# Token-major products in three passes instead of two, and the transposes of token block 1 a little later

## The chip, the core and the metric

The kernel runs on one core of one Trainium2 chip. The metric is device time in microseconds (us), from the first to the last instruction and what lies around them. Three runs of the kernel before took 1064.53, 1066.60 and 1066.75 us (median 1066.6).

## The reference

Two transformer blocks over 256 tokens of width 1024, in float32. The first has a gMLP mixer and a differential attention, each followed by a convolutional FFN; the second has a SwiGLU FFN, a mixer of MLA and block attention, and another SwiGLU FFN. Each of six stages begins with a normalised input that is multiplied by a weight:

```python
y = rmsnorm(h, norm_g[layer, 2])          # or rms_norm(x, g)
y = causal_dwconv(y @ w_up, conv_w, conv_b)   # or silu(y @ w_gate) * (y @ w_up), y @ w_in, ...
h = h + rmsnorm(y @ w_down, norm_g[layer, 3])
```

## The kernel before, in words

Tokens are in two blocks of 128 (tb 0 and 1). The weights come as 351 units of 128x1024 (512 KB each). Each float32 operand is split into a hi part and a lo part that TensorE takes at full speed, and a product is three matmuls: hi x hi (called HH here), hi x of the weights' lo (HL), and lo of x times hi of the weights (LH). A unit is prepared when it is called for: ScalarE writes its hi part `wh` (L304), VectorE its lo part `wl` (L310). `feed` prepares units ahead, up to W.ahead of them beyond those in use.

Between two stages lies `junction` (L573). For each token block it finishes the residual, forms the mean square, the norm `xn` (L510, two halves of 512 columns), turns `xn` on TensorE (L518, eight transposes into two tiles `pt`), and evicts the turned halves: ScalarE writes the hi part of `x` (L521), VectorE the lo part (L528). Token block 1 goes through this chain after token block 0, while TensorE already multiplies token block 0.

That multiplication is `token_major` (L409): the 8 chunks of 128 rows of x (k = 0 to 7) are the stationary operand, the weights stream, and the sums of one token block gather in two PSUM banks (`pz` in the FFNs, `accv` in the attention, `pmix` and `pckv` in the mixer). It returns a list of steps, one for each pass and each k, with a nominal time. `start` (L597) runs the steps of token block 0, then of token block 1, and calls `late` (the eight transposes of token block 1) at the first step at which the nominal time of the steps so far has reached TURN1.

Six stages begin in this way. They are numbered by their place in the trace: stage 1, the first FFN (82 us); stage 2, the differential attention (271 us); stage 3, the second FFN (382 us); stage 4, the third FFN (570 us); stage 5, the mixer (757 us); stage 6, the fourth FFN (869 us). An FFN's product is 768 columns wide, takes 6 units and 18 matmuls a pass; the attention's takes 8 units and 16 matmuls a pass; the mixer's 8 units and 16 matmuls a pass, then 2 more units for `pckv`. At the start of stages 2 and 5 six units are prepared, in stage 3 five of six, in stage 6, where W.ahead has been 4, two of six; the rest is prepared by instructions that stand behind the normalisation of token block 1 in ScalarE's and VectorE's queues.

Outside the stretches marked manual_schedule, as here, the order on each engine's queue is not that of the code: a planner places each instruction by its own estimate of when its inputs are ready, and the code's order only breaks ties. Instructions that write the same PSUM tile keep their order.

Of the kernel before, what the change touches and what calls it, by code (L numbers as in the profile page):

```python
# [56 lines left out]
k, v, q = (lambda c: ("k", c, 0)), (lambda tb: ("v", tb, 0)), (lambda h: ("q", h, 0))  # L57
# [172 lines left out]
def build(tc, nc, a, out):  # L230
    with ExitStack() as ctx:
        _build(ctx, tc, nc, a, out)


def _build(ctx, tc, nc, a, out):
# [10 lines left out]
    mm, act, vec = nc.tensor.matmul, nc.scalar.activation, nc.vector  # L246
# [121 lines left out]
    def block(x, tb, n=KD):  # L368

        return [(x[:, k, 0, TB[tb]], x[:, k, 1, TB[tb]]) for k in range(n)]  # L370
# [35 lines left out]
        vec.tensor_add(out_, hi, low)  # L406
        return out_

    def token_major(dst, xs, ws, n, major="pass"):  # L409

        last = len(xs) - 1
        res = []

        def one(k, passes):
            x = xs[k]
            segs = []
            for d, c0, c1 in dst:
                a0 = k * n + c0  # L420
                while a0 < k * n + c1:
                    a1 = min(k * n + c1, (a0 // D + 1) * D)
                    o = a0 - k * n - c0
                    segs.append((d[:, o:o + a1 - a0], a0 // D, slice(a0 % D, a0 % D + a1 - a0)))
                    a0 = a1
            for lr, hl in passes:
                for d, u, c in segs:
                    mm(out=d, lhsT=x[lr], rhs=ws(u)[hl][:, c], start=(k == 0 and lr == 0 and hl == 0), stop=(k == last and lr == 1))  # L428
        cols = sum(c1 - c0 for _, c0, c1 in dst)
        sets = ((((0, 0), (0, 1)), ((1, 0),)) if major == "pass" else (((0, 0), (0, 1), (1, 0)),))  # L430
        for passes in sets:
            for k in range(len(xs)):
                res.append((lambda k=k, passes=passes: one(k, passes), len(passes) * cols / 2400))
        return res
# [32 lines left out]
    def new_x():  # L467
        return xtp.tile([P, KD, 2, T], F32R, name=nm("x"), tag="x")
# [104 lines left out]
    def junction(proj, join, g):  # L573


        x = new_x()
        n0, n1 = [Norm(tb, proj.acc[tb], join, g, x) for tb in range(2)]
        n0.half(0, 1)
        n0.update()
        n0.scale()  # L580
        first, second = proj.rest()
        for f, _ in first:
            f()
        n1.half(0)
        cut_at = max(0.0, TURN0 - 0.64 * len(first))
        splice(second, [(cut_at, lambda: n0.turn(True))])
        n1.half(1)
        n1.update()
        n0.lo()
        n1.scale()  # L590
        return x, n1.turn

    QM = 2
    TURN0 = 7.0
    TURN1 = 5.0

    def start(x, late, groups):  # L597

        for tb in range(2):
            ops, done = groups(tb)  # L600
            t, turned = 0.0, tb == 1
            for f, us in ops:
                if not turned and t >= TURN1:
                    late()
# [10 lines left out]
    def ffn(x, late, evac, hooks):  # L615
# [6 lines left out]
        def groups(tb):  # L622
            pz = wide(tb, "pz")

            def done():
                zt = slot("z", shape=(P, n))
                for c0, c1 in parts:
                    act(zt[:, c0:c1], pz[c0 // 512][:, :c1 - c0], AF.Copy)
                z.append(zt)
            return token_major([(pz[c0 // 512][:, :c1 - c0], c0, c1) for c0, c1 in parts], block(x, tb), ws, n), done  # L630
# [240 lines left out]
    def diff_attention(x, late, bias, lam, sub, lam_work, mid):  # L871
# [3 lines left out]
        def groups(tb):  # L875
            acc = wide(tb, "accv")

            def done():
                vt = slot("vd")
                for q, c in enumerate(HALF):  # L880
                    act(vt[:, c], acc[q], AF.Copy)
                v.append(vt)
            return token_major([(acc[q], c.start, c.stop) for q, c in enumerate(HALF)], block(x, tb), ws, D), done
# [210 lines left out]
    def mixer(x, late, tables, mid):  # L1094
# [12 lines left out]
        def groups(tb):  # L1107
            pa = wide(tb, "pmix")
            pk = psm("pckv")
            ops = token_major([(pa[0], 0, 512), (pa[1][:, :416], 512, 928)], block(x, tb), w1, D)  # L1110
            ops += token_major([(pk[:, :T], 0, T)], block(x, tb), w2, T)

            def done():
                cn = slot("cn", shape=(P, 768))

                kr_, two = pa[1][:, 384:416], cn[:, 640:768].rearrange("p (r s d) -> p r s d", r=2, s=2)
                for s_, d, n, o in ((0, 0, 32, 0), (1, 0, 16, 16), (1, 16, 16, 0)):
                    vec.tensor_copy(two[:, :, s_, d:d + n], kr_[:, o:o + n].unsqueeze(1).to_broadcast([P, 2, n]))
                for ps, n, o in ((pa[1][:, :384], 384, 0), (pk[:, :T], 256, 384)):
                    ms = col("cms")  # L1120
                    act(cn[:, o:o + n], ps, AF.Square, accum_out=ms)
                    r = rsqrt_col(ms, mul=1.0 / n)
                    vec.scalar_tensor_tensor(out=cn[:, o:o + n], in0=ps, scalar=r, in1=cg[:, o:o + n], op0=ALU.mult, op1=ALU.mult)
                act(vals[1][:, tb, :], pa[0], AF.Copy)
                stage.append(cn)
            return ops, done
# [187 lines left out]
    x = new_x()  # L1314
# [5 lines left out]
    xs = [block(x, tb) for tb in range(2)]  # L1320
# [107 lines left out]
    x, late = junction(proj, held["post"], held["pre"])  # L1428
    hooks.append((MID, later(pre=lambda: norm_gain(1, 0), lam=lam_column, post=lambda: norm_gain(0, 3))))
    proj = ffn(x, late, conv_evac(held["cw"]), hooks)  # L1430
    x, late = junction(proj, held["post"], held["pre"])
    proj = diff_attention(x, late, rb["bias"], *held["lam"], later(pre=lambda: norm_gain(1, 2), cw=lambda: conv_taps(1), post=lambda: norm_gain(1, 1)))
    x, late = junction(proj, held["post"], held["pre"])
    proj = ffn(x, late, conv_evac(held["cw"]), [(MID, later(pre=lambda: gain(a["ffn1_norm"]), post=lambda: norm_gain(1, 3)))])
    x, late = junction(proj, held["post"], held["pre"])
    (step1, step2), tables = mixer_tables()
    proj = ffn(x, late, swiglu_evac, [(5, step1), (8, step2), (MID, later(pre=lambda: gain(a["mix_norm"]), cg=lambda: gain(a["cgain"], n=640)))])
    x, late = junction(proj, 0.5, held["pre"])
    proj = mixer(x, late, tables, later(pre=lambda: gain(a["ffn2_norm"])))
    x, late = junction(proj, 1.0, held["pre"])  # L1440
# [12 lines left out]
    for n, (c0, c1) in enumerate(ranges):  # L1453
        c, sum_ = slice(c0, c1), n < 2
# [16 lines left out]
    for c0, c1 in ranges[1:]:  # L1471
        c = slice(c0, c1)
# [47 lines left out]
```

## Time and profile before

| what | value |
|---|---|
| median of three runs (lowest, highest) | 1066.6 us (1064.53, 1066.75) |
| the profiled execution, its own time | 1064.43 us |
| span of that execution (first to last instruction) | 1062.6 us |
| TensorE busy in the span | 1047.2 us (99%) |
| TensorE's share of the chain that ended last | 93% |
| VectorE, ScalarE busy | 777.5 us (73%), 658.1 us (62%) |
| DMA, mean over the span | 185 GB/s |

The span and what lies around it make the execution's own time; the sum of the prediction is made against 1064.43. TensorE's busy time counts matmuls whose ends are modelled, so where one begins is better known than where it ends. An idle stretch of an engine is printed in brackets before the instruction that ended it, with the instruction that released it.

### The profile page before, as it was taken

To read this page: it belongs to the slowest core of one execution; us is meant where nothing else is said; L and a number is where in the kernel's file an instruction comes from. 1 tells how busy PE (TensorE), PEld (TensorE's weight loads), DVE (VectorE), ACT (ScalarE), POOL (GpSimd) and SP (SyncE) were. 2 spreads that over 40 slices of the span, in tenths; PEclk is the share of its full clock that TensorE was granted. 3 is DMA by queue.
4 is the path that set the end of the run, shared out by engine and by line. 5 is a ranking of instruction groups with operands and counts; after the bars stand their busy time and mean duration, and the time that the engine had idled before them with its cause. 6 is when DMAs were issued, how large, how long until landed. Compare 5 with 4: busy or idle time off the path is not lost.

```text
span 1062.6 us, 15791 instructions
## 1 busy us (share of the span) xinstructions
PE 1047.2 (99%) x5802; PEld 892.9 (84%) x5802; DVE 777.5 (73%) x1360; ACT 658.1 (62%) x1222; POOL 30.7 (3%) x57
## 2 busy tenths in 40 slices
PE   8999999999999999999999999999999999999997
PEld 6988888888788788888888888888898778888886
DVE  5886989887668877998876596665656867866633
ACT  6655867765578757876655575554457747755521
POOL 0100000000001110000001010000000000000000
PEclk9999999999999999999999999999999999999999
DMA  9956548653555446676534667564444456665501
GB/s 342 347 167 227 176 166 308 206 179 100 194 170 171 146 160 220 212 252 196 188 122 157 219 205 225 195 188 151 146 126 133 149 200 216 240 208 190 177 2 39
DMA packets 57246, 197.04 MB, mean 185 GB/s; under 512 B 6952, under 2 KB 9040, under 8 KB 57168
## 3 DMA queue, kind: packets, MB, share of 16 engines
q1 hardware_dynamic: 57024, 195.77, 55.8%
q8 instruction: 45, 0.74, 0.3%
q14 instruction: 33, 0.27, 0.1%
q10 hardware_dynamic: 144, 0.26, 0.1%
HBM read 194.94 MB, written 1.06 MB: 184 GB/s over the span
## 4 chain that ended last, share of the span: by engine, by line
PE 93%; DVE 2%; ACT 2%; DMA 1%; issue 1%; POOL 1%; SPq 0%; POOLq 0%; DVEq 0%; ACTq 0%
PE pu L385 26%; PE acc L544 26%; PE pu L384 12%; PE pz L428 5%; PE pq L385 4%; PE accv L1328 2%; PE pmix L428 2%; PE pq L384 2%; PE pu L387 2%; PE accv L428 2%; PE pt L518 1%; PE acc L1458 1%; PE pu L393 1%; PE pu L394 1%; PE pu L392 1%
## 5 line engine op out<-in xcount | busy, mean ns | idle before, releaser
L310 DVE TENSOR_TENSOR wl<-w,wh 128x1024 fp32r<-128x1024 f32 (+1 forms) x352 | 423.8, 1218 | 124.4 <-ACT wh L304 82.8
L385 PE MATMUL pu<-x,wh 128*128 128x512 f32 x1216 | 427.2, 396 | 0.0
L304 ACT ACTIVATE wh<-w 128x1024 fp32r<-128x1024 f32 (+1 forms) x352 | 362.1, 1051 | 94.2 <-DVE wl L310 62.9
L384 PE MATMUL pu<-x,wl 128*128 128x256 f32 x1064 | 296.7, 279 | 0.0
L385 PEld LDWEIGHTS pu<-x,wh 128*128 128x128 f32 x1216 | 222.7, 188 | 44.6 <-DVE y L682 0.6
L384 PEld LDWEIGHTS pu<-x,wl 128*128 128x128 f32 x1064 | 200.6, 189 | 6.6
L544 PE MATMUL acc<-wh,hh 128*128 128x512 f32 x434 | 145.4, 397 | 0.8 <-ACT hh L957 0.5
L544 PE MATMUL acc<-wl,hh 128*128 128x512 f32 x434 | 142.4, 390 | 0.0
L544 PE MATMUL acc<-wh,hl 128*128 128x512 f32 x434 | 141.4, 390 | 0.3 <-DVE hl L961 0.3
L399 ACT ACTIVATE low<-pu 128x256 f32<-128x256 f32 x152 | 57.4, 377 | 76.2 <-PE pu L385 75.3
L544 PEld LDWEIGHTS acc<-wh,hl 128*128 128x128 f32 x434 | 81.4, 188 | 18.3 <-DVE hl L961 0.9
L544 PEld LDWEIGHTS acc<-wl,hh 128*128 128x128 f32 x434 | 81.4, 188 | 17.0
L544 PEld LDWEIGHTS acc<-wh,hh 128*128 128x128 f32 x434 | 80.1, 188 | 16.1 <-ACT hh L437 1.4
L385 PE MATMUL pq<-x,wh 128*128 128x512 f32 x192 | 69.5, 403 | 0.0
L406 DVE TENSOR_TENSOR low<-pu,low 128x256 f32<-128x256 f32 x114 | 47.6, 418 | 17.8 <-ACT low L399 17.8
L428 PE MATMUL pz<-wh,x 128*128 128x256 f32 (+1 forms) x288 | 57.1, 321 | 0.0
L437 ACT ACTIVATE hh<-y 128x256 fp32r<-128x256 f32 x88 | 35.6, 409 | 29.8 <-DVE y L682 15.1
L670 ACT ACTIVATE y<-low,cw 128x256 f32<-128x256 f32 x76 | 45.0, 592 | 11.6 <-DVE low L406 11.2
L384 PE MATMUL pq<-x,wl 128*128 128x256 f32 x168 | 47.0, 279 | 0.0
L428 PEld LDWEIGHTS pz<-wh,x 128*128 128x128 f32 x288 | 42.5, 189 | 4.5 <-ACT x L521 0.3
L465 ACT ACTIVATE junk<-h 128x512 bf16<-128x512 f32 (+1 forms) x32 | 19.9, 622 | 40.3 <-DVE h L493 19.2
L438 DVE TENSOR_TENSOR hl<-y,hh 128x256 fp32r<-128x256 f32 x88 | 36.6, 420 | 9.8 <-ACT hh L437 9.7
(234 smaller groups left out, 1233.1 us busy)
## 6 DMA issues: line engine op xcount, KB each, us to landing
w<-in_wall SPq DMA_DIRECT2D x349, 512.0 KB, 4.4
gain<-in_norm_g SPq DMA_DIRECT2D x7, 512.0 KB, 6.7
h<-in_x SPq DMA_DIRECT2D x4, 256.0 KB, 5.5
w<-in_wall SPq DMA_DIRECT2D x4, 256.0 KB, 4.1
bias<-fd SPq DMA_DIRECT2D x2, 512.0 KB, 9.6
gain<-in_ffn_norm SPq DMA_DIRECT2D x2, 512.0 KB, 4.8
gain<-in_a_ln_g SPq DMA_DIRECT2D x1, 512.0 KB, 5.9
gain<-in_a_ln_b SPq DMA_DIRECT2D x1, 512.0 KB, 6.6
```

The lines of the kernel that those rows point to most:

```text
L304: act(self.hi[:, c], self.loaded[n][:, c], AF.Copy)
L310: vec.tensor_sub(wl[:, c], w[:, c], wh[:, c].bitcast(F32))
L384: mm(out=ps[:, T:], lhsT=wl, rhs=x[:, k, 0], start=False, stop=False)
L385: mm(out=ps, lhsT=wh, rhs=x[:, k], start=(k == 0), stop=(k == KD - 1))
L387: mm(out=ps[:, T:], lhsT=wl, rhs=x[:, k, 0], start=False, stop=False)
L399: act(low, ps[:, T:], AF.Copy)
L406: vec.tensor_add(out_, hi, low)
L428: mm(out=d, lhsT=x[lr], rhs=ws(u)[hl][:, c], start=(k == 0 and lr == 0 and hl == 0), stop=(k == last and lr == 1))
L437: act(hi, src, AF.Copy)
L438: vec.tensor_sub(lo, src, hi.bitcast(F32))
L544: mm(out=self.acc[tb][q], lhsT=hid[x][:, TB[tb]], rhs=w[hl][:, HALF[q]], start=s, stop=e)
L670: act(y, ps, AF.Identity, scale=cw[:, f, 2:3], bias=cw[:, f, 3:4])
```

## The change

The two sets of passes (HH and HL together for each k, then LH) become three: HH for all k, LH for all k, HL for all k. The flag that ends a sum goes to the last HL instead of the last LH. The unused argument of `token_major` goes. TURN1 goes from 5.0 to 5.5.

```diff
-    def token_major(dst, xs, ws, n, major="pass"):
+    def token_major(dst, xs, ws, n):
...
             for lr, hl in passes:
                 for d, u, c in segs:
-                    mm(out=d, lhsT=x[lr], rhs=ws(u)[hl][:, c], start=(k == 0 and lr == 0 and hl == 0), stop=(k == last and lr == 1))
+                    mm(out=d, lhsT=x[lr], rhs=ws(u)[hl][:, c], start=(k == 0 and lr == 0 and hl == 0), stop=(k == last and hl == 1))
         cols = sum(c1 - c0 for _, c0, c1 in dst)
-        sets = ((((0, 0), (0, 1)), ((1, 0),)) if major == "pass" else (((0, 0), (0, 1), (1, 0)),))
-        for passes in sets:
+        for passes in (((0, 0),), ((1, 0),), ((0, 1),)):
             for k in range(len(xs)):
                 res.append((lambda k=k, passes=passes: one(k, passes), len(passes) * cols / 2400))
...
-    TURN1 = 5.0
+    TURN1 = 5.5
```

A step now holds one pass over one k (nominally 0.32 us in an FFN, by `cols / 2400`), where a step of HH and HL held two. So the call of `late` moves, in the code, from behind 8 steps of 0.64 to behind 18 of 0.32 in the FFNs, from 6 of 0.853 to 13 of 0.427 in the attention, and from 7 of 0.773 to 15 of 0.387 in the mixer. In the three kinds of stage that is 0.64, 0.43 and 0.39 us of nominal work later. Where the transposes come in TensorE's queue is the planner's choice. Before, it followed the code in stages 1, 2, 4 and 5. Now it does so in stages 1 and 4 alone: before behind 36 matmuls (HH and HL of all k), now behind 41 (HH, LH and the first 5 of HL).

TensorE's queue in stage 2, around the transposes of token block 1 (`pt`, from `xn`); `accv` with an even and an odd number are the two halves of the columns, a `wh` or `wl` is one unit. Before, behind 24 matmuls (HH and HL for k = 0 to 5):

```order
L428 MATMUL accv_2960<-wl_602_2834,x_2851 128x512
L428 MATMUL accv_2961<-wl_602_2834,x_2851 128x512
L428 MATMUL accv_2960<-wh_604_2847,x_2851 128x512
L428 MATMUL accv_2961<-wh_604_2847,x_2851 128x512
L428 MATMUL accv_2960<-wl_605_2849,x_2851 128x512
L428 MATMUL accv_2961<-wl_605_2849,x_2851 128x512
L518 MATMUL pt_2986<-ident,xn_2957 128x128 x4
L518 MATMUL pt_2987<-ident,xn_2957 128x128 x4
L428 MATMUL accv_2960<-wh_638_3002,x_2851 128x512
```

Now, behind 12 (HH alone, for k = 0 to 5), with HH of k = 6 (the seventh unit, `wh_636`) between the third and the fourth transpose:

```order
L428 MATMUL accv_2960<-wh_601_2832,x_2851 128x512
L428 MATMUL accv_2961<-wh_601_2832,x_2851 128x512
L428 MATMUL accv_2960<-wh_604_2847,x_2851 128x512
L428 MATMUL accv_2961<-wh_604_2847,x_2851 128x512
L517 MATMUL pt_3000<-ident,xn_2957 128x128 x3
L428 MATMUL accv_2960<-wh_636_2976,x_2851 128x512
L428 MATMUL accv_2961<-wh_636_2976,x_2851 128x512
L517 MATMUL pt_3000<-ident,xn_2957 128x128
L517 MATMUL pt_3001<-ident,xn_2957 128x128 x4
L428 MATMUL accv_2960<-wh_639_2984,x_2851 128x512
```

The transposes stand 12 matmuls earlier in the queue than before. Stage 5 has the same pattern: before behind 28 matmuls of `pmix`, now three of them behind 12, and the rest two matmuls later.

TensorE's queue in stage 3, in the same place; `wh_949` is the hi part of the sixth unit. Before, behind 30 matmuls of `pz`:

```order
L428 MATMUL pz_4194<-wh_914_4073,x_4091 128x512
L428 MATMUL pz_4194<-wl_915_4075,x_4091 128x512
L518 MATMUL pt_4238<-ident,xn_4191 128x128 x3
L428 MATMUL pz_4195<-wh_949_4227,x_4091 128x256
L428 MATMUL pz_4194<-wh_949_4227,x_4091 128x512
L518 MATMUL pt_4238<-ident,xn_4191 128x128
L518 MATMUL pt_4239<-ident,xn_4191 128x128 x4
L428 MATMUL pz_4195<-wl_950_4229,x_4091 128x256
```

Now, the first three behind 15; the other five come 26 matmuls later, behind the rest of HH, all of LH and 5 of HL:

```order
L428 MATMUL pz_4195<-wh_914_4073,x_4091 128x256
L428 MATMUL pz_4194<-wh_914_4073,x_4091 128x512
L517 MATMUL pt_4243<-ident,xn_4191 128x128 x3
L428 MATMUL pz_4195<-wh_949_4213,x_4091 128x256
L428 MATMUL pz_4194<-wh_949_4213,x_4091 128x512
L428 MATMUL pz_4195<-wh_949_4213,x_4091 128x256
L428 MATMUL pz_4194<-wh_868_3908,x_4091 128x512
```

The first three transposes have moved 15 matmuls towards the front of the queue.

TensorE's queue in stage 6 now, where two units are prepared at the start (`wh_1989`, `wh_1995`); `pz_9194` and `pz_9195` are token block 0, `pz_9329` and `pz_9330` token block 1:

```order
L428 MATMUL pz_9194<-wh_1995_9104,x_9115 128x256
L428 MATMUL pz_9195<-wh_1995_9104,x_9115 128x256
L428 MATMUL pz_9194<-wh_1995_9104,x_9115 128x512
L517 MATMUL pt_9263<-ident,xn_9191 128x128 x4
L517 MATMUL pt_9264<-ident,xn_9191 128x128 x4
L428 MATMUL pz_9329<-wh_1989_9075,x_9115 128x512
L428 MATMUL pz_9330<-wh_1989_9075,x_9115 128x256
```

They stand behind 6 matmuls of HH; before, behind 12 (the same 6 and 6 of HL). Behind them now come 6 of HH for token block 1 and then, unit by unit, 3 of token block 0 and 3 of token block 1 for the third, fourth and fifth unit, with HL of both blocks last; before, HH and HL of each unit stood side by side.

ScalarE's and VectorE's queues in these stages keep their order but for two places: in stage 3 two preparations (L304, L310) now stand ahead of the evictions of token block 1 (L521, L528), and in stage 5 one stands behind them. From stage 6 on, some evictions of the fourth FFN change places with a neighbour. POOL's and SP's queues keep their order.

## Rows read from the trace of the kernel before

**Rows 1.** The page: busy time, share of the span and instructions of each engine.

```profile
PE 1047.2 (99%) x5802; PEld 892.9 (84%) x5802; DVE 777.5 (73%) x1360; ACT 658.1 (62%) x1222; POOL 30.7 (3%) x57
```

**Rows 2.** The waits of TensorE in the whole span: who waited for whom, us in total, times, the longest.

```profile
PE pt L518 <- DVE xn L510: 4.7, 6, 1.6
...
PE pz L428 <- DVE wl L310: 0.4, 1, 0.4
```

**Rows 3.** The time line of TensorE in stage 2: start, us, instruction, count, and in brackets the idle time before it.

```profile
270.80 0.62 PE L428 MATMUL accv<-wh,x 128*128 128x512 f32 x2
...
273.52 0.62 PE L428 MATMUL accv<-wh,x 128*128 128x512 f32 x2
...
275.79 0.61 PE L428 MATMUL accv<-wl,x 128*128 128x512 f32 x2
276.86 1.29 PE L518 MATMUL pt<-ident,xn 128*128 128x128 f32 x8 [0.46 <-DVE xn L510]
```

**Rows 4.** The time line of ScalarE, then of VectorE, in stage 2.

```profile
274.96 1.99 ACT L304 ACTIVATE wh<-w 128x1024 fp32r<-128x1024 f32 x2
...
275.96 1.41 DVE L510 SCALAR_TENSOR_TENSOR xn<-h,rs_r,gain 128x512 f32<-128x512 f32 x2 [0.66 <-POOL rs_r L460]
```

**Rows 5.** The time line of TensorE in stage 3.

```profile
381.56 0.50 PE L428 MATMUL pz<-wh,x 128*128 128x512 f32 x2
...
386.04 0.40 PE L428 MATMUL pz<-wl,x 128*128 128x512 f32 x1
387.54 0.55 PE L518 MATMUL pt<-ident,xn 128*128 128x128 f32 x3 [1.10 <-DVE xn L510]
387.84 0.60 PE L428 MATMUL pz<-wh,x 128*128 128x256 f32 x2
...
389.33 0.39 PE L428 MATMUL pz<-wl,x 128*128 128x256 f32 x1 [0.35 <-DVE wl L310]
```

**Rows 6.** The time line of ScalarE, then of VectorE, in stage 3.

```profile
385.72 1.99 ACT L304 ACTIVATE wh<-w 128x1024 fp32r<-128x1024 f32 x2
...
386.73 1.41 DVE L510 SCALAR_TENSOR_TENSOR xn<-h,rs_r,gain 128x512 f32<-128x512 f32 x2 [0.66 <-POOL rs_r L460]
```

**Rows 7.** The time line of stage 5: TensorE, ScalarE, VectorE.

```profile
757.39 0.57 PE L428 MATMUL pmix<-wh,x 128*128 128x512 f32 x2
...
759.91 0.58 PE L428 MATMUL pmix<-wh,x 128*128 128x512 f32 x2
...
763.28 1.04 PE L518 MATMUL pt<-ident,xn 128*128 128x128 f32 x8
...
759.01 2.94 ACT L304 ACTIVATE wh<-w 128x1024 fp32r<-128x1024 f32 x3
...
760.01 1.41 DVE L510 SCALAR_TENSOR_TENSOR xn<-h,rs_r,gain 128x512 f32<-128x512 f32 x2 [0.67 <-POOL rs_r L460]
```

**Rows 8.** The time line of stage 6: TensorE, ScalarE, VectorE.

```profile
868.62 0.50 PE L428 MATMUL pz<-wh,x 128*128 128x512 f32 x2
...
870.27 0.40 PE L428 MATMUL pz<-wl,x 128*128 128x512 f32 x1
872.29 1.29 PE L518 MATMUL pt<-ident,xn 128*128 128x128 f32 x8 [1.63 <-DVE xn L510]
873.61 0.61 PE L428 MATMUL pz<-wh,x 128*128 128x512 f32 x2
...
873.45 1.05 ACT L304 ACTIVATE wh<-w 128x1024 fp32r<-128x1024 f32 x1
...
874.88 8.64 ACT L304 ACTIVATE wh<-w 128x1024 fp32r<-128x1024 f32 x9
...
871.39 1.41 DVE L510 SCALAR_TENSOR_TENSOR xn<-h,rs_r,gain 128x512 f32<-128x512 f32 x2 [0.73 <-POOL rs_r L460]
```

**Rows 9.** The time line of TensorE: the transposes of token block 0 in stage 1, then the end of HH and HL of token block 0 and the transposes of token block 1, in stage 1 and in stage 4.

```profile
80.96 0.63 PE L518 MATMUL pt<-ident,xn 128*128 128x128 f32 x4 [1.04 <-DVE xn L510]
...
87.89 0.51 PE L428 MATMUL pz<-wl,x 128*128 128x512 f32 x2
88.62 1.29 PE L518 MATMUL pt<-ident,xn 128*128 128x128 f32 x8 [0.22 <-DVE xn L510]
...
575.72 0.51 PE L428 MATMUL pz<-wl,x 128*128 128x512 f32 x2
576.49 1.29 PE L518 MATMUL pt<-ident,xn 128*128 128x128 f32 x8 [0.26 <-DVE xn L510]
```

**Rows 10.** The time line of stage 1: VectorE's lo parts of x for token block 0, and ScalarE's hi parts of x for token block 1.

```profile
82.26 1.36 DVE L528 TENSOR_TENSOR x<-pt,x 128x512 fp32r<-128x512 f32 x2 [0.18 <-ACT x L521]
...
89.28 1.26 ACT L521 ACTIVATE x<-pt 128x512 fp32r<-128x512 f32 x2 [0.58 <-PE pt L518]
```

**Rows 11.** The instructions of L428: operation, count, shortest, median and longest duration in ns, first and last start, form.

```profile
L428 PEld LDWEIGHTS pz<-wh,x x288: 186/188/192, 82.3 to 888.4; 128*128 128x128 f32 x144
...
L428 PEld LDWEIGHTS pz<-wl,x x144: 186/188/192, 82.8 to 885.6; 128*128 128x128 f32 x144
```

**Rows 12.** Busy time by stretch: the stretch, its length, busy us and instructions of PE, PEld, DVE, ACT and POOL, then TensorE's granted clock (1.00 is its full speed), DMA share and GB/s. The wait in stage 6, and two stretches at the end of the program.

```profile
870.67:872.29 1.62, 0.00 (x0) 0.03 (x1) 0.90 (x2) 0.00 (x0) 0.55 (x1) 1.00 0.85 349
1058.00:1060.00 2.00, 0.00 (x0) 0.00 (x0) 0.88 (x2) 0.72 (x1) 0.40 (x1) 1.00 0.10 32
1060.00:1062.60 2.60, 0.00 (x0) 0.00 (x0) 0.00 (x0) 0.00 (x0) 0.00 (x0) 0.51 0.47 177
```

## The prediction

> **What bounds the kernel.** I read the page first: TensorE is busy 1047.2 of 1062.6 us [rows 1]. So hardly anything counts but the gaps on TensorE, and the next view is the list of its waits [rows 2]. The transposes of L518 waited for `xn` six times, 4.7 us in all, the longest 1.6 us, and L428 once for a lo part, 0.4 us. These are the only waits that the change can touch. The third view is the time line of each of the six stages; the reader is to see in it when TensorE comes to the transposes of token block 1 and when `xn` lets them start. The fourth is the order of the queues in the changed program, because the time line shows that the queue is kept. In stage 3 the transposes stand as three, two matmuls, then five, and so they run: after 1.10 us of idling, three transposes at 387.54, then the matmuls, though the hi part which these need came from a conversion that began at 385.72 [rows 5, 6].
>
> **What the change does not move.** The matmuls are the same in number and shape. `xn` of token block 1 comes from VectorE, ScalarE and POOL, whose order up to there is unchanged and which wait for nothing in the product of token block 0. So the transposes cannot start earlier than now: every matmul that leaves the front of them is idle time, and every one that comes in front of them fills idle time. From the start of the second norm to the first transpose takes 0.90 us in stage 2 (275.96 to 276.86) [rows 3, 4] and 0.90 us in stage 6 (871.39 to 872.29) [rows 8].
>
> **Stages 1 and 4: a gain.** The queue puts 5 more matmuls (0.70 us by the spacing below) ahead of the transposes. The last two before them start at 87.89 and at 575.72; two of 256 and 512 columns take some 0.35 us to the next start, so TensorE was free at 88.24 and 576.07 and lost 0.38 and 0.42 us [rows 9]. Both are less than 0.70, so both go: **-0.8 us**. What could be late next is x of token block 1: its evictions begin at 89.28, 0.66 us after the first transpose [rows 9, 10], and 13 matmuls of HL (some 2 us) still lie ahead of its first user. LH, now second, begins where the last 18 of the 36 matmuls did, some 2.8 us (18 at 0.157) before 88.24, and the lo parts of token block 0 that it needs are done at 83.68 [rows 10]. In the other stages the transposes move to the front, and x of token block 1 with them.
>
> **Stage 2: a loss.** Before, 24 matmuls lie ahead; the first starts at 270.80, the thirteenth at 273.52, the last pair at 275.79 [rows 3]. Now only 12 lie ahead, so TensorE comes to the transposes at 273.52 and waits to 276.86. The 12 others (2.72 us) come later, when nothing is left to hide: **+2.7 us**. HH of the seventh unit, between the transposes, is free of waits: two hi parts are converted from 274.96 in 1.99 us [rows 4].
>
> **Stage 3: a loss.** 30 matmuls run from 381.56 to about 386.27 (the last starts at 386.04) [rows 5], 4.71 us; half of them now lie ahead of the first three transposes: TensorE comes to these at 383.9 instead, and they start at 387.54 as before: **+2.35 us**. The wait of 0.35 us for the sixth lo part goes, because HL is last: **-0.35 us** [rows 5]. The hi part of that unit, wanted directly behind the three transposes, is ready (two conversions from 385.72, 1.99 us) [rows 6]. The five transposes that now come 26 matmuls later have their `xn` long since. The two conversions that pass the evictions on ScalarE and VectorE cost nothing, for those evictions wait for the late fifth to eighth transposes anyway.
>
> **Stage 5: a loss.** Before there is no wait at 763.28 [rows 7]. Now TensorE comes to the transposes behind 12 matmuls, at 759.91; the second norm begins at 760.01 and releases them 0.90 us on, at 760.91: **+1.0 us**. The seventh and eighth hi parts are converted from 759.01 on, three in 2.94 us, and meet their matmuls [rows 7].
>
> **Stage 6: a loss, and a new wait.** 12 matmuls run from 868.62 to about 870.50, of which 6 now stand ahead: half of 1.88 us is added to the idle 1.63 us, **+0.94 us** [rows 8]. Behind the transposes (to 873.6) come 6 matmuls of token block 1 (0.94 us, to 874.55), for which the third unit's hi part is done at 874.50; its 6 matmuls run to 875.48. The next three hi parts are done at 875.93, 876.88 and 877.83 (nine from 874.88 in 8.64 us, 1.05 us the last, so 0.95 us apart) and each feeds 6 matmuls of 0.93 us: TensorE waits 0.45 us for the first and next to nothing for the others, **+0.5 us**. Before, HH and HL of a unit took twice as long, which hid this. By its bounds this term is between 0 (a hi part somewhat earlier) and 1.5 us (all three late by as much).
>
> **What is not seen.** In token block 1 the lo parts of the shared units are now read to the end, so buffers for later weights come free later, by at most the 2.9 us of one pass. Nothing in the rows prices that; the bound below is 0, above it is one wait like the 0.4 us for a lo part [rows 2] in each of four FFNs, 1.6 us. I take 0, for the wait list has no wait behind such a load in these stretches.
>
> At the weight loads a rule speaks against the change. The rows: 288 loads of x for 288 matmuls with `wh` and 144 for 144 with `wl`, 188 ns each at the median [rows 11]; a second matmul with the same chunk of x loads it again, so parting HH from HL costs no load: 0. The Trainium skill, TensorE: Matmul & The Clock Gate, section on what each phase is for, says that weights are to be loaded once and multiplied repeatedly. By it, HL as a pass of its own would want 8 more loads for each token block of a stage, 96 in all, some 18 us by an estimate with 188 ns, were none hidden; the trace disagrees with its premise here.
>
> **The sum.** -0.8 + 2.7 + 2.35 - 0.35 + 1.0 + 0.94 + 0.5 = +6.3 us. On the profiled execution's 1064.4 us that is 1070.7. The median shown, 1066.6, lies 2.2 us above that execution, and one of the three runs beside it; a new median can fall in either place, 1070.7 or 1072.9, and I take **1072.0**.
>
> **The rivals.**
> *TensorE goes on past a waiting transpose.* Then the places in the queue mean little, the matmuls behind fill the gaps, and what decides is whether 0.4 us or more of work is ready when the transposes are not. The waits for `xn` of token block 1 would shrink to nothing: -3.7 us (4.7 less 1.04 for token block 0 in stage 1 [rows 2, 9]) and -0.4, that is 1060.3, faster. For it: such work is in the queue in all six stages. Against it: in stage 3 TensorE idled 1.10 us with a matmul behind the transposes whose hi part was done at about 386.8 [rows 5, 6]. 5 in 100.
> *TensorE's clock falls in the longer gaps.* The gaps of stages 2 and 3 come to 3.3 and 3.6 us, twice the longest now. In the rows the clock stays at its full 2.4 GHz through the idle 1.6 us of stage 6 and still in 1058 to 1060, when the last matmul is over, and reads 0.51, that is 1.2 GHz, in the last 2.6 us, in which TensorE did nothing either [rows 12]. At the lower level the matmuls behind a gap take twice as long; no row shows how long that lasts. Between 0 and doubling the 7.7 us that token block 0 has left in stage 2 (34 matmuls of 0.227), I put 3 us on each of two gaps: 1078. The same page of the skill, section on why this matters for your kernels, warns of idle gaps between bursts of matmuls, behind which the clock is lower; in the gaps of this trace that does not show. 5 in 100.
> *The change does not do what its words say, yet costs nothing,* because `xn` is not what ends the waits: were the transposes released by TensorE's own earlier work, they would move with it. Then only small terms are left, within 2 us of 1066.6. Against it: each wait ends 0.90 us behind the second norm's start. 6 in 100.
> *More waits for weights* in stage 6 and for buffers, at the upper bounds: +2.6 us more, 1074.6. 9 in 100.
>
> **How the numbers follow.** My forecast has 75 in 100. A measurement tells 0.2%, 2.1 us, from no change. Slower by more: 75 + 5 + 9 = 89. Within: 6. Faster: 5. For the range: the terms that rest on a row each way are good to some 0.7 us in all, the median's place to 2.2 us, so the forecast alone lies between 1069.5 and 1074; taking in the bounds above, 1069.0 to 1075.5. The clock, the second rival, is left out of it, and so are most of the two milder ones.
>
> **What would show it.** Right: the wait of L518 for `xn` grows from 4.7 to about 11 us in all, in four long pieces (about 3.2 in stage 2, 3.5 in stage 3, 0.9 in stage 5, 2.6 in stage 6), with 1.0 left in stage 1 and none in stage 4; the wait of L428 for a lo part is gone, and one of some 0.5 us for a hi part stands in stage 6. TensorE's busy time stays near 1047. Wrong: transposes that start earlier than 0.9 us behind the second norm, matmuls that run between the arrival at the transposes and their start, or a granted clock under 1.00 behind a gap.

## The result, and the profile after

The changed kernel takes **1074.3 us** (median of four runs, 1072.87 to 1076.22) beside 1065.6 of the kernel before on the same chip. The ratio is 1.0082, 95% interval 1.0070 to 1.0094: slower by 8.7 us. The forecast was 1072.0, its range 1069.0 to 1075.5. The profiled execution took 1072.87 us, its span is 1071.1; before, 1064.43 and 1062.6.

The page first. TensorE's row, to be held against [rows 1]:

```profile
PE 1050.2 (98%) x5802; PEld 897.1 (84%) x5802; DVE 777.7 (73%) x1360; ACT 657.0 (61%) x1222; POOL 31.8 (3%) x57
```

The span grew by 8.5 us and TensorE's busy time by 3.0, with as many instructions; so 5.5 us are idle time and 3.0 are matmuls that took longer. The waits of TensorE (us in total, times, the longest) show the first part:

```profile
PE pt L517 <- DVE xn L509: 11.1, 5, 3.5
```

11.1 us instead of the 4.7 of [rows 2], and the wait for a lo part is gone from the list. The time line of TensorE shows where: stage 1 (the view ends after the first four matmuls of HL), then stages 2, 3, 5 and 6 (L517 is L518 of before; the idle time ahead of an instruction is in brackets).

```profile
88.45 1.03 PE L517 MATMUL pt<-ident,xn 128*128 128x128 f32 x8
89.24 0.95 PE L428 MATMUL pz<-wl,x 128*128 128x512 f32 x4
...
269.67 2.88 PE L428 MATMUL accv<-wh,x 128*128 128x512 f32 x12
275.74 0.87 PE L517 MATMUL pt<-ident,xn 128*128 128x128 f32 x3 [3.18 <-DVE xn L509]
276.26 1.20 PE L428 MATMUL accv<-wh,x 128*128 128x512 f32 x2
...
384.04 2.51 PE L428 MATMUL pz<-wh,x 128*128 128x512 f32 x15
390.01 0.55 PE L517 MATMUL pt<-ident,xn 128*128 128x128 f32 x3 [3.45 <-DVE xn L509]
390.31 5.06 PE L428 MATMUL pz<-wh,x 128*128 128x256 f32 x21
...
765.99 0.52 PE L517 MATMUL pt<-ident,xn 128*128 128x128 f32 x3 [0.84 <-DVE xn L509]
...
878.40 1.52 PE L517 MATMUL pt<-ident,xn 128*128 128x128 f32 x8 [2.59 <-DVE xn L509]
879.71 8.70 PE L428 MATMUL pz<-wh,x 128*128 128x512 f32 x45
```

The idle pieces in stages 2, 3, 5 and 6 are 3.18, 3.45, 0.84 and 2.59 us; the forecast had 3.2, 3.5, 0.9 and 2.6. What the forecast did not have is the pace behind them. In stage 3 the 21 matmuls take 5.06 us, where 0.157 each would be some 3.5 with the end of the last. The stretches say why (stretch, its length, TensorE's busy us and instructions, granted clock, DMA share, GB/s):

```profile
274.00:275.00 1.00, 0.00 (x0) 1.00 0.46 160
275.00:276.00 1.00, 0.27 (x2) 0.58 0.85 315
276.00:277.00 1.00, 1.00 (x5) 0.50 0.34 139
...
390.00:391.00 1.00, 0.99 (x7) 1.00 0.00 0
391.00:392.00 1.00, 1.00 (x7) 0.60 0.00 0
392.00:393.00 1.00, 1.00 (x5) 0.50 0.00 0
393.00:394.00 1.00, 1.00 (x6) 0.50 0.37 45
394.00:395.00 1.00, 1.00 (x6) 0.69 0.52 193
395.00:396.00 1.00, 1.00 (x9) 1.00 0.74 299
```

The granted clock goes from 1.00 to 0.50, that is from 2.4 to 1.2 GHz, inside the gap of stage 2 (TensorE starts again at 275.74) and 1.2 us behind the gap of stage 3, and comes back. Stage 6 shows the same (0.50 in 880 to 882, 0.82 in 882 to 884). In the profile of before nothing of the kind stands behind a gap of these stages.

A table of my own condenses the time lines. For each execution it has the time from the first matmul of token block 0 to the first instruction behind the whole product, in us, by stage:

| profiled execution | 1 | 2 | 3 | 4 | 5 | 6 | sum |
|---|---|---|---|---|---|---|---|
| before | 18.53 | 23.76 | 19.76 | 18.54 | 26.85 | 20.14 | 127.6 |
| after | 17.87 | 27.39 | 23.04 | 17.88 | 27.88 | 22.47 | 136.5 |
| e1, the passes alone | 18.55 | 26.07 | 23.08 | 18.54 | 27.89 | 22.23 | 136.4 |
| e2, TURN1 alone | 17.88 | 24.11 | 19.81 | 17.88 | 27.00 | 21.68 | 128.4 |
| e3, gaps filled | 17.90 | 26.02 | 21.54 | 17.88 | 27.88 | 21.52 | 132.7 |
| e4, HH and LH paired | 17.85 | 23.11 | 19.17 | 17.83 | 26.84 | 20.14 | 124.9 |
| e5, all three per k | 17.78 | 23.10 | 17.82 | 17.87 | 26.84 | 19.21 | 122.6 |
| e6, order of the code | 17.89 | 27.02 | 20.88 | 17.88 | 27.67 | 21.94 | 133.3 |
| e7, eight units ahead | 17.94 | 24.14 | 17.87 | 17.88 | 26.96 | 20.18 | 125.0 |
| e9, before with a filled gap | 18.53 | 23.79 | 19.81 | 18.54 | 26.84 | 19.91 | 127.4 |

From before to after the six products grow by 8.95 us. Between them nothing moved: from the end of one to the start of the next it is 169.71, 87.00, 169.10, 168.43 and 84.38 us before, and 169.73, 86.98, 169.08, 168.43 and 84.37 after. (The first stage began 0.5 us earlier in the profiled execution of after, which makes 8.5.)

### The profile page after: what moved, and what is told of

Same layout as the page of the kernel before. It is cut to its first block, busy times and chain, and to the rows that moved or that the text cites. A ratio compares the mean times of both kernels' runs of the same rounds, so it can differ in the third digit from the quotient of the medians.

```text
span 1071.1 us, 15789 instructions
## 1 busy us (share of the span) xinstructions
PE 1050.2 (98%) x5802; PEld 897.1 (84%) x5802; DVE 777.7 (73%) x1360; ACT 657.0 (61%) x1222; POOL 31.8 (3%) x57
## 4 chain that ended last, share of the span: by engine, by line
PE 94%; DVE 2%; ACT 2%; POOL 1%; issue 1%; DMA 0%; SPq 0%; POOLq 0%; DVEq 0%; ACTq 0%
PE pu L385 26%; PE acc L543 26%; PE pu L384 12%; PE pz L428 6%; PE pq L385 4%; PE accv L1327 2%; PE accv L428 2%; PE pq L384 2%; PE pmix L428 2%; PE pu L387 2%; PE pt L517 1%; PE acc L1457 1%; PE pu L393 1%; PE pu L392 1%; PE pu L394 1%; ACT junk L464 1%
## 5 line engine op out<-in xcount | busy, mean ns | idle before, releaser
L310 DVE TENSOR_TENSOR wl<-w,wh 128x1024 fp32r<-128x1024 f32 (+1 forms) x352 | 423.9, 1219 | 128.9 <-ACT wh L304 88.5
L304 ACT ACTIVATE wh<-w 128x1024 fp32r<-128x1024 f32 (+1 forms) x352 | 361.9, 1051 | 97.5 <-DVE wl L310 63.9
L543 PE MATMUL acc<-wh,hh 128*128 128x512 f32 x434 | 145.4, 397 | 0.8 <-ACT hh L956 0.5
L543 PE MATMUL acc<-wl,hh 128*128 128x512 f32 x434 | 142.4, 390 | 0.0
L543 PE MATMUL acc<-wh,hl 128*128 128x512 f32 x434 | 141.4, 390 | 0.3 <-DVE hl L960 0.3
L543 PEld LDWEIGHTS acc<-wh,hl 128*128 128x128 f32 x434 | 81.4, 188 | 18.2 <-DVE hl L960 0.9
L543 PEld LDWEIGHTS acc<-wl,hh 128*128 128x128 f32 x434 | 81.4, 188 | 17.0
L543 PEld LDWEIGHTS acc<-wh,hh 128*128 128x128 f32 x434 | 80.1, 188 | 16.1 <-ACT hh L436 1.4
L428 PE MATMUL pz<-wh,x 128*128 128x256 f32 (+1 forms) x288 | 50.0, 334 | 0.0
L428 PEld LDWEIGHTS pz<-wh,x 128*128 128x128 f32 x288 | 43.7, 201 | 5.0 <-ACT x L520 0.2
L464 ACT ACTIVATE junk<-h 128x512 bf16<-128x512 f32 (+1 forms) x32 | 19.9, 622 | 40.3 <-DVE h L492 19.2
```

Source lines behind the costliest of these rows:

```text
L304: act(self.hi[:, c], self.loaded[n][:, c], AF.Copy)
L310: vec.tensor_sub(wl[:, c], w[:, c], wh[:, c].bitcast(F32))
L464: act(junk[:, :src.shape[-1]], src, AF.Square, scale=1.0 / 32.0, accum_out=ms)
L543: mm(out=self.acc[tb][q], lhsT=hid[x][:, TB[tb]], rhs=w[hl][:, HALF[q]], start=s, stop=e)
```

## The experiments

My theory: the loss is idle time in front of the transposes, because three passes ask for prepared units twice as fast (HH alone is done with a unit after 3 matmuls in an FFN, HH and HL after 6) and the planner then puts the transposes forward; and on top of it matmuls at the lower clock behind those gaps. e1, e3, e4, e5, e6 and e7 are edits of the changed kernel, e2 and e9 of the kernel before. The rivals: that TURN1 carries a part, that HL last costs by itself, that the slow matmuls are slow for another reason, that only the planner's choice of place costs.

**e1, the passes without TURN1.**

```diff
-    TURN1 = 5.5
+    TURN1 = 5.0
```

> The three passes alone, TURN1 at 5.0 as before. In stages 2, 3, 5 and 6 the queue of TensorE is the same as with the whole change (transposes behind 12, 15, 12 and 6 matmuls); in stages 1 and 4 they stand behind 36 matmuls instead of 41 (before 32). Theory (the passes ask for units twice as fast, and the planner therefore puts the transposes forward): the same waits of 3.2, 3.5, 0.8 and 2.6 us in stages 2, 3, 5 and 6; in stages 1 and 4 four more matmuls than before, 4 x 0.157 = 0.63 us, still cover the 0.38 and 0.42 us that were lost, so no wait there: within 1 us of the whole change, about 1074. Rival (the two steps of TURN1 carry a good part of the loss): 1069 to 1071, and shorter waits in stages 2 and 3.

Measured: 1074.9 us beside 1066.2, ratio 1.0078 (1.0064 to 1.0092), the same as the whole change within the intervals. Stages 2, 3, 5 and 6 have the same idle pieces to 0.01 us, so TURN1 has no part in the loss. On stages 1 and 4 the expectation miscounted: 36 matmuls stood ahead of the transposes before too, so nothing changed there, and 18.55 and 18.54 us are the times of before. One line of stage 2 and the stretches around it (columns as above):

```profile
277.68 0.52 PE L517 MATMUL pt<-ident,xn 128*128 128x128 f32 x3 [3.18 <-DVE xn L509]
```

```profile
276.00:278.00 2.00, 0.32 (x4) 1.00 0.83 293
278.00:280.00 2.00, 2.00 (x14) 1.00 0.05 16
```

The same gap of 3.18 us, and this time the clock stays at 1.00. So stage 2 gives the price of the idle time alone, 26.07 - 23.76 = +2.3 us, and that of a fall of the clock, 27.39 - 26.07 = 1.3 us.

**e2, TURN1 without the passes.**

```diff
-    TURN1 = 5.0
+    TURN1 = 5.5
```

> TURN1 at 5.5 alone, with the two sets of passes of before. The transposes stand behind 37 matmuls instead of 32 in stages 1 and 4, behind 26 instead of 24 in stage 2 (five of the eight, then two HL, then three), behind 32 instead of 28 in stage 5, and where they were in stages 3 and 6. Theory: the waits of about 0.4 us in each of stages 1, 2 and 4 go, those of 1.1 us (stage 3) and 1.6 us (stage 6) stay: -1.2 us, about 1064.4 against 1065.6, with the wait for xn at 3.7 us in all instead of 4.7. Rival (moving the transposes back makes x of token block 1 late): a new wait at the first matmul of token block 1 and no gain, 1065.6 or more.

Measured: 1064.9 us, ratio 0.9990 (0.9981 to 0.9999), about the -1.2 us expected. (The count of 32 is the same slip, it was 36.) Stages 1 and 4 each give 0.65 us: what the change gains there comes from TURN1. In stage 2 the wait for `xn` goes but a new one of 0.74 us for a lo part of the seventh unit appears, and the stage is 0.35 us slower. Stage 6, with the same queue and the same gap as before, took 1.5 us more. Its line, and the stretches:

```profile
871.27 1.29 PE L518 MATMUL pt<-ident,xn 128*128 128x128 f32 x8 [1.63 <-DVE xn L510]
```

```profile
872.00:874.00 2.00, 1.98 (x10) 0.73 0.41 137
874.00:876.00 2.00, 2.00 (x9) 0.50 0.34 131
876.00:878.00 2.00, 2.00 (x13) 0.92 0.28 39
```

The clock fell behind a gap of 1.63 us, as long as the one in [rows 8] behind which it had stayed at 1.00.

**e3, the change with the gaps filled.**

```diff
             self.los = []
+            for _ in range(FILL[stage[0]] if self.tb else 0):
+                nc.tensor.transpose(pt[0][:, :P], ident, ident)
...
+    FILL = {1: 0, 2: 16, 3: 20, 4: 0, 5: 0, 6: 14}
...
+        stage[0] += 1
```

> The whole change, and ahead of the transposes of token block 1 16, 20 and 14 transposes of the identity in stages 2, 3 and 6, into the tile that the real ones then overwrite. At 0.11 us each they should take 1.8, 2.2 and 1.5 us of the idle 3.18, 3.45 and 2.59 us, in the same place of the queue; nothing that the output needs comes earlier or later by them. Theory (the clock falls behind the long gaps, and that is the 3 us by which TensorE is busier than before): idle stretches of about 1.4, 1.2 and 1.1 us are left, shorter than the 1.63 us of stage 6 before, behind which the clock stayed at 1.00; the granted clock stays at 1.00, the matmuls behind the gaps run at their usual spacing, and the time falls by about 3 us, to 1071.3. Rival (the matmuls behind the gaps are slow for another cause, such as the burst of conversions beside them): nothing changes, 1074.3, and stage 3 still takes 4.9 us for its 21 matmuls.

Measured: 1070.6 us, ratio 1.0041 (1.0029 to 1.0054): 3.7 us under the median of the change (4.4 by the two ratios to the kernel before), while the transposes start, to 0.1 us, as long after the first matmul of their stage as in the change. The time line of stages 2, 3 and 6, then two of the stretches:

```profile
276.18 0.55 PE L521 MATMUL pt<-ident,xn 128*128 128x128 f32 x3 [1.34 <-DVE xn L511]
...
389.21 0.55 PE L521 MATMUL pt<-ident,xn 128*128 128x128 f32 x3 [1.27 <-DVE xn L511]
389.51 3.53 PE L428 MATMUL pz<-wh,x 128*128 128x256 f32 x21
...
876.02 1.38 PE L521 MATMUL pt<-ident,xn 128*128 128x128 f32 x8 [0.95 <-DVE xn L511]
...
879.75 5.43 PE L428 MATMUL pz<-wh,x 128*128 128x512 f32 x33 [0.23 <-ACT wh L304]
```

```profile
277.00:279.00 2.00, 2.00 (x13) 1.00 0.13 33
...
390.00:392.00 2.00, 2.00 (x15) 1.00 0.00 0
```

The 21 matmuls of stage 3 are back at 3.5 us, the clock reads 1.00 behind all three gaps, and stages 2, 3 and 6 are 1.37, 1.50 and 0.95 us shorter. The rival (another cause for the slow matmuls) falls: the five runs of e3 (1069.64 to 1071.71) all lie below the four of the change. With the matmuls at full pace a wait for a hi part appears in stage 6, 0.23 us, which the slow matmuls of the changed kernel had hidden.

**e4, HL last, but HH and LH paired.** Units are asked for at the old rate.

```diff
-        for passes in (((0, 0),), ((1, 0),), ((0, 1),)):
-            for k in range(len(xs)):
-                res.append((lambda k=k, passes=passes: one(k, passes), len(passes) * cols / 2400))
+        for lr, hl, k in [(0, 0, 0), (0, 0, 1), (1, 0, 0), (1, 0, 1)] + [(lr, 0, k) for k in range(2, len(xs)) for lr in (0, 1)] + [(0, 1, k) for k in range(len(xs))]:
+                res.append((lambda k=k, p=(lr, hl): one(k, (p,)), cols / 2400))
```

> TURN1 at 5.5, and the lo parts of the weights last as in the change, but HH and LH of each k together (for the first two k HH of both, then LH of both), then HL of all k. So units are asked for at the old rate. The transposes stand behind 41, 26, 30, 41, 30 and 12 matmuls in stages 1 to 6 (before: 32, 24, 30, 32, 28, 12; with the change: 41, 12, 15, 41, 12, 6). Theory (the rate at which units are asked for is what costs): the waits of stages 1, 2 and 4 go, those of 1.1 and 1.6 us in stages 3 and 6 stay, the 0.35 us for a lo part goes: -1.6 us from 1065.6, about 1064.0; granted clock 1.00. Rival (it is the lo parts last, which keep buffers of the shared units to the end and load x twice, that cost): slower than before, 1069 or more.

Measured: 1062.25 us, ratio 0.9967 (0.9956 to 0.9979): faster than before by about 3.5 us. The lo parts of the weights come last here too, and no wait stands where the rival wants one. In the profile the six products shorten by 2.6 us, one more than expected: stages 1, 2 and 4 by 0.65 to 0.71 each (a wait gone gives more than its idle time, see below; in stages 1 and 4 that is TURN1's gain, as in e2), stage 3 by 0.59.

**e5, all three of a k together.** Units are asked for at two thirds of the old rate.

```diff
...
+        for lr, hl, k in [(0, 0, 0), (0, 1, 0), (0, 0, 1), (0, 1, 1), (1, 0, 0), (1, 0, 1)] + [(lr, hl, k) for k in range(2, len(xs)) for lr, hl in ((0, 0), (0, 1), (1, 0))]:
...
```

> TURN1 at 5.5, and HH, HL and LH of each k together (for the first two k LH last of both), so that units are asked for at two thirds of the old rate. The transposes stand behind 41 or 42 matmuls in stages 1, 3 and 4 (36, 30 and 36 before), behind 26 in stage 2 (24), 30 in stage 5 (28) and 18 in stage 6 (12). Theory (what costs is the rate at which units are asked for; at a lower rate the planner has more to put ahead of the transposes): the products of stages 1 and 4 shorten by 0.65 us each as they did with the change, stage 2 by 0.65, stage 3 loses its idle 1.10 and the 0.35 for a lo part, 1.45 in all, stage 5 stays, stage 6 has 6 more matmuls ahead, 0.94: -4.3 us from the profiled 1064.4, about 1060 at the same place in the spread, 1061 to 1062 at the median. Rival (lo parts wanted at once, as the two waits for wl with TURN1 alone, 0.7 and 0.4 us, suggest): new waits for wl take back what the transposes give, 1064 or more.

Measured: **1059.7 us**, ratio 0.9943 (0.9931 to 0.9956): 6 us faster than before, some 14.6 faster than the change, the fastest of all, and 1.3 us or more below the 1061 to 1062 expected of the median. (The flag that ends a sum is back on the last LH; the line that adds the step is that of e4.) TensorE in stages 3 and 6:

```profile
386.82 1.03 PE L516 MATMUL pt<-ident,xn 128*128 128x128 f32 x8
...
868.57 1.29 PE L516 MATMUL pt<-ident,xn 128*128 128x128 f32 x8 [0.68 <-DVE xn L508]
```

The 1.10 us of stage 3 are gone, of the 1.63 of stage 6 0.68 are left, and no wait for a lo part shows in the list. The products shorten by 4.96 us, expected 4.3; 1.4 of it lie in stages 1 and 4, where TURN1 alone gives 1.3 (e2).

**e6, the change in the order of the code.** TensorE's queue is not left to the planner.

```diff
     def start(x, late, groups):
-        for tb in range(2):
+        with tc.manual_schedule(engines={mybir.EngineType.PE}):
+          for tb in range(2):
...
```

> The whole change with TensorE's queue in the six starts in the order of the code: the transposes of token block 1 stand behind 41 matmuls in the FFNs, 26 in stage 2 and 30 in stage 5; the conversions of the units are put ahead of the evictions of token block 1. Theory (the units are not prepared early enough for HH alone, wherever the transposes stand): TensorE now waits for hi parts instead of xn, 2.4 and 0.5 us in stage 2 (12 HH are over at 273.5 by the times of before, the next two hi parts come at 275.95 and 276.95), about 2.9 in stage 3, 0.6 in stage 5 and 2.0 in stage 6, some 8.4 us instead of 10.1: 1072 to 1074, still far above before. Rival (only the place that the planner gave the transposes costs): with them back behind 26 to 41 matmuls the waits go, 1066 or less.

Measured: 1072.6 us, ratio 1.0064 (1.0048 to 1.0080), as the theory had it. (The rest of the edit is the loop's body, two columns further in.) The waits of TensorE, three of the list:

```profile
PE pz L428 <- ACT wh L304: 4.7, 3, 2.7
PE accv L428 <- ACT wh L304: 2.4, 1, 2.4
...
PE pt L517 <- DVE xn L509: 1.0, 1, 1.0
```

Of the waits for `xn` only that of token block 0 in stage 1 is left, and TensorE waits for hi parts instead: 2.4 us in stage 2, 2.7 in stage 3, 0.3 in stage 5, 1.9 in stage 6. So the place that the planner chose is the smaller part of the loss: with the code's place 7.3 us of waiting (8.4 expected) are left of the 10.1, and with falls of the clock in stages 2 and 6 the six products are 3.2 us shorter than with the change, still 5.7 longer than before. HH alone comes to units that are not there.

**e7, eight units prepared ahead.**

```diff
-AHEAD = 6
+AHEAD = 8
```

> The whole change with AHEAD = 8 instead of 6, so that up to eight units are prepared ahead in nearly all of the kernel; the 36 slots are the same, so weights are loaded later in places. The transposes stand behind 41, 26, 41, 41, 30 and 12 matmuls in stages 1 to 6, where the code puts them. Theory (passes cost only where units are not ready): no wait for xn in stages 2 to 5, the products of stages 1 to 5 as short as or shorter than before (17.9, 23.1, 18.3, 17.9 and 26.9 us), stage 6 as before with its 1.63 us. If the slots suffice that is some 1062 to 1064; what the later loads cost elsewhere is not known and may exceed it. Rival (three passes cost by themselves, for instance by buffers kept to the end): the products stay above those of before even with the transposes at their place.

Measured: 1071.15 us, ratio 1.0048 (1.0033 to 1.0064). The products are what the theory says, but for stage 2 (24.14 us, expected 23.1), which begins at the lower clock: their sum is 125.0 us, 2.6 under before, and stage 3 is at 17.87 us with three passes. The total is slow for what the deeper preparation costs elsewhere: 5.8 us between products 1 and 2, 2.5 ahead of stage 1 (with a fall of the clock there) and 1.2 around stage 5. TensorE, then VectorE, ahead of stage 2:

```profile
276.65 1.97 PE L517 MATMUL pt<-ident,xn 128*128 128x128 f32 x8 [4.39 <-DVE xn L509]
```

```profile
267.99 1.23 DVE L310 TENSOR_TENSOR wl<-w,wh 128x1024 fp32r<-128x1024 f32 x1 [6.07 <-PE acc L543]
...
272.10 1.41 DVE L502 SCALAR_TENSOR_TENSOR h<-t,rs_r,h 128x512 f32<-128x512 f32 x2
```

In VectorE's queue a preparation (L310) now stands ahead of the residual of token block 0 (L502) and waits 6.07 us for TensorE's last products (L543); the norm of token block 0 comes late behind it, and TensorE idles 4.39 us. From the end of product 1 to the start of product 2 it is 175.5 us instead of 169.7. The clock was low there too, 0.50 from 276 to 280.

**e8, the kernel before again, for its clock.** No edit.

> The kernel before, once more, for its clock. With TURN1 alone the same idle stretch of 1.63 us in stage 6 was followed by 3.3 us at a granted clock of 0.50, where the profile of before reads 1.00. Theory (behind a gap of that length the clock falls in some executions only, and this makes the spread of 2 us between the runs of one kernel): an execution of 1064.5 shows 1.00 behind all gaps, one of 1066.5 shows a stretch near 0.50 behind a gap of stage 3 or 6, and PE busy 1048 to 1049 instead of 1047.2. Rival (the spread has nothing to do with it): 1.00 everywhere in an execution of 1066.5 too.

Measured: 1067.17 us, TensorE busy 1049.9. Two stretches of lower clock: in 8 to 12 us (0.57) and behind the gap of stage 6:

```profile
873.45 1.29 PE L518 MATMUL pt<-ident,xn 128*128 128x128 f32 x8 [1.63 <-DVE xn L510]
```

```profile
8.00:12.00 4.00, 3.99 (x16) 0.57 1.04 417
...
874.00:876.00 2.00, 1.94 (x10) 0.80 0.46 100
876.00:878.00 2.00, 2.00 (x10) 0.50 0.44 168
```

This execution is 2.74 us longer than the one profiled at first and TensorE is busy 2.7 us longer: 1.6 us of it lie in stage 6, 1.0 ahead of stage 1. One kernel, one gap, two outcomes.

**e9, the kernel before with the gap of stage 6 filled.**

```diff
...
+    FILL = {1: 0, 2: 0, 3: 0, 4: 0, 5: 0, 6: 11}
...
```

> The kernel before, with 11 transposes of the identity ahead of the transposes of token block 1 in stage 6, where they should take 1.2 of the idle 1.63 us and leave about 0.4. Nothing else moves. Theory (behind the 1.63 us the clock falls in part of the executions, 3.4 us at the lower level and 1.7 us lost each time, and that is most of the spread): no fall behind the gap of stage 6 in the profile, the product of stage 6 at 20.1 us, and the median of the runs 0.5 to 1.5 us below that of before, about 1065; single runs may still hold a fall in the first 12 us. Rival (the spread is from elsewhere): the median stays at 1066, within 0.3 us of before.

(The other lines are those of e3.)

Measured: 1065.0 us, ratio 0.9998 (0.9989 to 1.0007). In its profile no fall stands behind the gap, which is down to 0.34 us, and stage 6 takes 19.9 us; but a fall stands in the first 12 us. The median did not move (the interval leaves room for a gain of 1.2 us), and twelve runs still spread from 1064.23 to 1067.19 us, so the rival holds on that point: falls behind the gap of stage 6 are not what makes most of the spread between runs. What does is open, but the profiles point at the program's start: the first matmul of stage 1 begins at 82.56 us in the first profile of before, 83.53 in e8 and 84.14 in e9, the two with a fall in the first 12 us, and in the other profiles without e7 anywhere from 82.07 (after) to 83.91 (e6).

## Why the prediction was right, point by point

*What bounds the kernel, and what the change does not move.* Right. All of the difference lies in the six products, and the transposes that were moved forward wait there for `xn`. One reading was off, without weight for the sum: in stage 3 the wait ends 0.81 us behind the second norm's start (386.73 to 387.54 [rows 5, 6]), not 0.90.

*Stages 1 and 4.* Forecast -0.8, measured -0.66 each, -1.3. The idle time of 0.38 and 0.42 us was right, but eight transposes that had to wait are slower as well: from their start to the next matmul's it is 1.04 us before (88.62 [rows 9] to 89.66) and 0.79 after (88.45 to 89.24).

```profile
89.66 1.54 PE L428 MATMUL pz<-wh,x 128*128 128x512 f32 x8
```

The single instructions in the trace of before show why: the second half of `xn` is done at 89.13, and the fifth transpose, the first that needs it, starts at 89.28, 0.31 us behind the fourth, where the others in that row of eight follow at 0.11 to 0.14. e1 and e2 show that TURN1 gives all of it.

*Stage 2.* Forecast +2.7, measured +2.3 where the clock stayed up (e1, e3), +3.6 in the profiled execution of after. The 12 matmuls that moved are 2.72 us, of which 0.4 came back behind the gap. Half of that is seen: three transposes, two matmuls and five transposes take 1.28 us in e1 (277.68 to 278.96), eight waiting transposes (1.04) and two matmuls (0.45) 1.49. The other half is a wait too short for the list [rows 2]: before, the first two matmuls with the seventh unit's lo part start 0.35 and 0.34 us behind the one ahead of them (at 278.56 and 278.90) instead of 0.23. That lo part is done at 278.51, and with HL last e1 has no such place.

*Stage 3.* Forecast +2.0 with the lost wait for the lo part; +1.8 with the clock up (e3), +3.3 in after.

*Stage 5.* Forecast +1.0; measured +1.03.

*Stage 6.* Forecast +0.94 and +0.5; +1.4 with the clock up (e3), of which 0.23 are the wait for a hi part; +2.3 in after, where slower matmuls hide that wait. This mechanism was right and half as large, and in after it did not show as the wait that was forecast.

*Buffers and weight loads.* Both taken as 0. The times between the products are the same to 0.1 us, and there are 5802 loads for 5802 matmuls before and after.

The sum of these is +6.3 in the forecast and +5.2 with the clock up (e3). The rest is **the clock**, the step that failed: 5 in 100 were put on it, it was kept out of the range, and TensorE's busy time was to stay near 1047, where it is 1050.2. A granted clock under 1.00 behind a gap was one of its own signs of being wrong, and it came. The working looked at one gap of 1.63 us behind which the clock read 1.00 and took that for a rule [rows 8, 12]; e2 and e8 show the fall behind the same gap. The other sign stood in its rows: the 0.51 at the end of the program. Two stretches of before, then two of after (columns as above):

```profile
1056.00:1057.00 1.00, 0.72 (x7) 1.00 0.00 0
1060.00:1061.00 1.00, 0.00 (x0) 0.53 0.97 371
...
1065.00:1066.00 1.00, 0.15 (x2) 1.00 0.00 0
1067.00:1068.00 1.00, 0.00 (x0) 0.52 0.00 0
```

The last matmul of before ends at 1056.72, and the clock falls some 3.3 us behind it; gaps of 3.3 and 3.6 us were forecast. In after it falls only some 1.9 us behind the last matmul, so neither time is a bound.

By the stages of after and e3 the clock costs 3.8 us (1.37 + 1.50 + 0.95), by their medians 3.7. The size that the rival gave to a fall, 3 us, was more than twice what one cost (1.3 on the mean of the three). The forecast came within 2.3 us all the same, since its other terms were 1.1 us too high together; the 1.3 us that it put on the sum for the place of the median were about right (1.4). That the time lies well inside the range is in part luck, of two errors that went against each other: with those 1.1 us on top it would be 1075.4, at the edge.

The Trainium skill, TensorE: Matmul & The Clock Gate, section on why this matters for your kernels, warns of idle gaps between bursts of matmuls. The prediction held the trace of before against that; the runs after agree in part, with falls behind gaps of 1.63 us (e2, e8) and none behind 3.18 (e1). Its section on what is actually happening says that the point of change is not tied to the kernel's start and varies from run to run; it says so of the rise, and the gap of 3.18 us with a fall in after and without one in e1 fits that. What the prediction made a rule, loading once and multiplying repeatedly, that page gives as what a separate load allows.

The other rivals: TensorE does not pass a waiting transpose (nothing runs in the gaps); `xn` is what ends the waits; in the six stages of after no wait for a weight is left, and in e3 one of 0.23 us.

## What to carry to other kernels

The order of passes sets how fast prepared operands are used up: at a start with few units ready, give each unit all its products before the next one is asked for (e5), and let the planner have that work to put in front of whatever waits. Price a gap on TensorE twice, as idle time and as a possible stretch at the lower clock behind it, and do not conclude from one execution without a fall that there is none. More units prepared ahead also take the loss away where the matmuls stand, but cost more elsewhere here (e7). Look first at where an instruction ends up in the queue: a step moved back in the code here came forward by 12, 15, 16 and 6 matmuls in stages 2, 3, 5 and 6.

## What the runs showed of the hardware that was not expected

The falls of the clock within the program lost the same amount: summed over 1 us stretches, the granted clock was 1.70 us short of full in stages 2, 3 and 6 of after, in stages 3 and 6 of e1, in stages 2 and 6 of e6, in stage 6 of e2 and of e8, and in the first 12 us of e7, e8 and e9; e7 lost twice that, 3.41 us, in and behind its gap of 4.39. What it costs is less where part of the low stretch is still idle time (stage 2: 1.3 us).

Whether it falls is not settled by the gap's length in these runs: 3.18 us with and without, 1.63 us with (e2, e8) and without (before, e7), 2.74 us without (stage 3 of e6), 2.37 and 1.71 us with (stages 2 and 6 of e6). Behind gaps of 1.34 us and less in these stages no fall was seen, but that is no safe length: in the first 12 us of e8 it went from 1.00 to 0.50 behind gaps of 0.81 and 0.79 us. It may also begin 1.2 us after the matmuls have resumed, as in stage 3 of after.
